# Layer norms with ScalarE's square root and one Newton step, narrower cross scores, a reordered opening and a last block in column pieces

## The chip, the cores and the metric

The kernel runs on 1 core of one Trainium2 chip (trn2). The metric is the device time of one execution in microseconds (us); several executions are taken and their median is given. All tensors are float32 in memory. A matrix product of two float32 operands is made from split operands: a high part `h` rounded to the type float32r, and a low part `l`, the remainder. Three products of float32r (h·h, h·l, l·h) are accumulated in PSUM.

## The reference

A trunk of two post-norm layers over 512 positions of width 1024. Layer 0 mixes tokens with gated linear attention (GLA), layer 1 with gated DeltaNet (GDN); behind each mixer stands a gated feed-forward block with a short causal convolution. After every one of these four sublayers comes a residual and a layer norm:

```python
def layer_norm(x, g, b):
    mu = jnp.mean(xf, -1, keepdims=True)
    var = jnp.mean(jnp.square(xf - mu), -1, keepdims=True)
    return ((xf - mu) * lax.rsqrt(var + LN_EPS)).astype(x.dtype) * g + b
...
    h = layer_norm(ALPHA * h + y, ln_g[i, 0], ln_b[i, 0])
    h = layer_norm(ALPHA * h + conv_ffn(h, ffn_w_in[i], ffn_conv_w[i], ffn_w_out[i]),
                   ln_g[i, 1], ln_b[i, 1])
```

In GLA (4 heads, key width 128, value width 256) the positions are cut into chunks of 64, and the scores of a chunk are `q * exp(b - b_ref)` times `k * exp(b_ref - b)`, causal. The kernel works on pairs of chunks (128 positions), so it also needs the cross scores: queries of the second 64 positions of a pair with keys of the first 64.

## The kernel before

The class `Trunk` holds everything. Positions are cut into 4 blocks of 128 (`tb` 0 to 3, NTB = 4), the width into 8 chunks of 128 (NC = 8) or into two halves of 512 (`hf`, S = 512). The activations lie transposed in `xh` and `xl` (128 partitions x 8 chunks x 512 positions).

**Weights.** `plan` is a list of weight items in the order of their use. `prefetch` issues items up to `look` ahead of the one in use: a DMA on SyncE's queue into one of 3 `raw` buffers, a cast on ScalarE (`wh`, L257), the remainder on VectorE (`wl`, L258). `fm_items` makes products whose outputs have features on the partitions (PSUM tile `fm`), `tm_half` those with positions on the partitions (PSUM tile `tm`): for each pair of weight chunks it goes over the 4 blocks, and the last `tail` pairs it does block by block, so that block 0 is finished while blocks 1 to 3 are still to come. `done` (L393 or L395) then adds the product to the residual `h`, takes the statistics of that half (L400), and after the second half starts the layer norm of the block.

**The order of the work.** The functions are Python generators that are started by `spawn` with a delay and advanced by `pump` between matmuls, on a clock `clk` that the code keeps itself. The framework then orders each engine's instructions by this order and their dependences. `keep_in_program_order` fixes the order of TensorE's instructions until the first mixer's projections are made (`pin`); `behind` puts one instruction after another on the same engine without a wait. `table` chains the activations that need a certain function table of ScalarE in one order, and `exp_ln_table` loads a table ahead of its first use.

**The layer norm.** `ln_stats` (L532 to L546) aggregates the statistics (L534), computes half the variance plus epsilon (L536), a first guess of 1/sqrt by integer instructions (L541, L542), and three Newton steps of two 128x1 instructions (L544, L545). All of it runs on VectorE. `ln` is used by the first three norms: it scales one half of the block on ScalarE (L558) and one on VectorE (L559); TensorE transposes the result (tile `xT`, L175), ScalarE applies gain and bias (`xf`, L568) and the high and low parts are written (L572, L575, L576). `ln_out` is used by the last norm: centering and gain (L600), scaling and bias (L601), the output DMA on SyncE (L602).

**The opening.** `load_x` loads x: blocks 0 and 1 at once on SyncE's and ScalarE's queues, blocks 2 and 3 on ScalarE's queue behind the casts of blocks 0 and 1. TensorE makes 2 constant products (L484) while it waits, transposes blocks 0 and 1 (`x_parts`), and makes 3 more. `fm_items` starts with HEADSTART = 4 weight items on the first 256 positions (blocks 0 and 1), then the same 4 on the other 256. The third of the 4 items is the `rep` item, 16 columns of the gate's low rank (L267, L272, L273). The task `second` transposes blocks 2 and 3 in between. The constants (the norms' weight rows `gla_nw` L728 and `gdn_nw` L938, spread over the partitions, and many small rows, L453) go through GpSimd's queue.

**The cross scores** are made in `core` (L844, tile `sx`): per head and pair of chunks a product of 64 keys with all 128 queries of the pair, of which the columns 64 to 127 are used.

Of the kernel before, what the change touches and what calls it, by code (L numbers as in the profile page):

```python
# [15 lines left out]
P = 128  # L16
# [36 lines left out]
class Trunk:  # L53
# [3 lines left out]
    def __init__(self, ctx, tc):  # L57
        self.tc = tc
        self.nc = nc = tc.nc
        self.n = 0  # L60
        ec = ctx.enter_context
        ap = ec(tc.tile_pool(name="acts", bufs=1))
        self.xh = ap.tile([P, NC, S], F32R, name="xh", tag="xh")
        self.xl = ap.tile([P, NC, S], F32R, name="xl", tag="xl")
        self.wp = ec(tc.tile_pool(name="wts", bufs=WB))
        self.mp = ec(tc.tile_pool(name="mem", bufs=SLOTS))
        self.rp = ec(tc.tile_pool(name="raws", bufs=RAWB))
        self.cp = ec(tc.tile_pool(name="const", bufs=1))
# [6 lines left out]
        self.one, self.warm = ones[:, 0:1], ones[:, 1:2]  # L75
        nc.gpsimd.memset(ones, 1.0)
        self.reset = self.keep([P, S], "reset")
# [9 lines left out]
        self.after = None  # L87
# [8 lines left out]
        self.next_block = 0.0  # L96


# [119 lines left out]
    def issue(self, item):  # L218
# [6 lines left out]
        if item[0] == "fm":  # L225
            _, w, col = item
            nc.sync.dma_start(
                raw.rearrange("p (c f) -> p c f", c=NC),
                w[:, col:col + P].rearrange("(c p) f -> p c f", p=P))
        elif item[0] == "tm":  # L230
# [24 lines left out]
        for n in (S, used) if self.issued == 0 else (used,):  # L255
            cols = slice(0 if n < used or self.issued else S, n)
            nc.scalar.copy(wh[:, cols], raw[:, cols])  # L257
            nc.vector.tensor_sub(wl[:, cols], raw[:, cols], wh[:, cols])  # L258
        self.vec(1.24)
        return [(wh[:, blk(j, S)], wl[:, blk(j, S)]) for j in range(used // S)]  # L260

    def issue_rep(self, w, col):
# [8 lines left out]
        src = r3.unsqueeze(2).to_broadcast([P, NC, 3, 16])  # L271
        nc.scalar.copy(w5[:, :, :, 0, :], src)  # L272
        nc.vector.tensor_sub(w5[:, :, :, 1, :], src, w5[:, :, :, 0, :])  # L273
        return wt

    def prefetch(self):
        while self.issued < min(len(self.plan), self.taken + self.look):
            item = self.plan[self.issued]
            if self.held == WB and not self.in_slots(item):
                break  # L280
            if self.after is None:
                self.ready.append(self.issue(item))
            else:
                with self.tc.issue_after(self.after):
                    self.ready.append(self.issue(item))
                self.after = None
            self.issued += 1
# [67 lines left out]

    def tm_half(self, a, n, tail, done, slots=False):

        npair = (n + 1) // 2
        ps = [self.psum("tm") for _ in range(NTB)]

        def terms(tb, cp, w):
            for j in range(min(2, n - 2 * cp)):
                c = 2 * cp + j
                self.tm_terms(ps[tb], *a(c, tb), *w[j], c == 0, c == n - 1)
            self.pump()
# [7 lines left out]
        for tb in range(NTB):  # L373
            for i in range(tail):
                terms(tb, npair - tail + i, ws[i])
                if tb == NTB - 1 and not slots:
                    self.spend()
            done(tb, ps[tb])

# [3 lines left out]

    def out_proj(self, a, n, first, final):

        nc = self.nc
        self.st = [None] * NTB
        for hf in range(2):
            def done(tb, ps, hf=hf):
                h = self.h[tb][hf]  # L390
                if first:
# [5 lines left out]
                if final is not None:  # L397
                    if hf == 0:
                        self.st[tb] = self.small([P, 2, 6], "ln_st")
                    nc.vector.bn_stats(self.st[tb][:, hf, :], h)  # L400
                    self.vec(0.7)
                    if hf == 1:
# [6 lines left out]
            self.tm_half(a, n, TAIL if last else 1, done, last)  # L409
        self.look = LOOKAHEAD  # L410
# [19 lines left out]
    def split_out(self, dst_h, dst_l, src):  # L430
        cast = self.nc.scalar.copy(dst_h, src)  # L431
        self.nc.vector.tensor_sub(dst_l, src, dst_h)
        return cast

# [27 lines left out]

    def x_parts(self, tb):
        for hf in range(2):
            ps = self.psum("xT")
            self.tr4(ps, self.h[tb][hf])
            xs = (slice(None), slice(4 * hf, 4 * hf + 4), blk(tb))
            cast = self.split_out(self.xh[xs], self.xl[xs], c4(ps))
        self.set(("x", tb))
        return cast.ins  # L470

    def load_x(self, x):
# [18 lines left out]
        constant(2)  # L491
        for tb in range(2):
            cast = self.x_parts(tb)
        constant(3)
        with self.tc.issue_after(cast):
            for tb in range(2, NTB):
                load(nc.scalar, tb)
            self.prefetch()

        def second():  # L500
            for tb in range(2, NTB):
                self.after = self.x_parts(tb)
                yield 1.2
            self.look = LOOKAHEAD

        self.spawn(second(), 4.0)

# [22 lines left out]

    def ln_stats(self, tb):
        nc = self.nc  # L532
        mv = self.small([P, 2], "ln_mv")
        nc.vector.bn_aggr(mv, self.st[tb])  # L534
        hv = self.small([P, 1], "ln_var")
        nc.vector.tensor_scalar(hv, mv[:, 1:2], LN_EPS, 0.5, op0=ALU.add, op1=ALU.mult)  # L536

        rs = self.small([P, 1], "ln_rs")
        t = self.small([P, 1], "ln_t")
        ri = rs.bitcast(I32)  # L540
        nc.vector.tensor_single_scalar(ri, hv.bitcast(I32), 1, op=ALU.logical_shift_right)  # L541
        nc.vector.tensor_scalar(ri, ri, -1.0, float(0x5F3759DF - 0x400000 - (1 << 31)), op0=ALU.mult, op1=ALU.add)  # L542
        for _ in range(3):
            nc.vector.scalar_tensor_tensor(t, rs, hv, rs, ALU.mult, ALU.mult)  # L544
            nc.vector.scalar_tensor_tensor(rs, t, 1.5, rs, ALU.subtract, ALU.mult)  # L545
        self.vec(2.2)  # L546
        return mv, rs
# [47 lines left out]
    def ln_out(self, tb, out):  # L595
        nc = self.nc
        gb, h = self.ln_gb(), self.h[tb]
        mv, rs = self.ln_stats(tb)
        for hf in range(2):
            nc.vector.scalar_tensor_tensor(h[hf], h[hf], mv[:, 0:1], gb[hf], ALU.subtract, ALU.mult)  # L600
            nc.vector.scalar_tensor_tensor(h[hf], h[hf], rs, gb[2 + hf], ALU.mult, ALU.add)  # L601
            nc.sync.dma_start(out[blk(tb), blk(hf, S)], h[hf])  # L602
        yield 0.0
# [49 lines left out]
    def ffn(self, cw, li, g, b, final, out=False):  # L653
        nc = self.nc
        for ci, (f0, f1) in enumerate(CHUNKS):
# [22 lines left out]
            a = lambda c, tb: (gs[c][0][:, blk(tb)], gs[c][1][:, blk(tb)])  # L678
            self.out_proj(a, f1 - f0, ci == 0, final if last else None)

# [37 lines left out]
    def gla_consts(self, w_gk2, b_gk, norm_w):  # L718
# [19 lines left out]
        self.b_gk = self.keep([P, 4], "gla_b")  # L738
        self.spawn(self.columns([(b_gk.rearrange("(n p) -> n p", p=P), 4, self.b_gk)]), 1.0)

    def gla(self, li, g, b):
# [89 lines left out]
        def core(hd):  # L831
# [101 lines left out]
    def gdn_consts(self, conv_w, a_log, dt_bias, norm_w):  # L933
# [460 lines left out]
```

## Time and profile before

| | |
|---|---|
| Median of 3 runs | 1286.5 us (1286.39 to 1287.05) |
| The profiled execution's own time | 1286.57 us |
| Its span, first to last instruction | 1284.5 us |
| TensorE busy (PE) | 1267.5 us, 99% |
| VectorE busy (DVE) | 794.2 us, 62% |
| ScalarE busy (ACT) | 543.8 us, 42% |
| GpSimd busy (POOL) | 111.1 us, 9% |
| Mean DMA rate | 99 GB/s |

Times in the profile count from the start of the span. A row of a timeline has the start, the length, the engine, the line of the kernel, the operation, what it writes and reads, and in brackets how long the engine was idle before it and what ended that. A "q" behind an engine's name means its sequencer, which issues DMAs (SPq, ACTq). A row of groups has the count, then the busy time, the mean length of one in ns, and the engine's idle time ahead of them. A row of the chain has the start, the time until the chain's next piece, and the count. One product of plain float32 operands appears as two matmul records (`sx`, `V`, the constant products), one of float32r operands as one. Matmuls overlap in the pipeline, so a matmul's length is not its cost: the pace is the distance from one start to the next.

### The profile page before, as it was taken

What the parts mean: (1) busy time and instruction counts of PE and PEld (TensorE: products, weight loads), DVE (VectorE), ACT (ScalarE), POOL (GpSimd) and SP (SyncE); (2) the same over time, 40 slices, a digit from 0 to 9 for tenths busy, and PEclk for the clock granted to TensorE, in tenths of its full rate; (3) what the DMA queues carried; (4) which work ended last, traced back from release to release, by engine and by line L of the source; (5) the groups of instructions that cost most, each with busy time, mean ns of one, the idle gap of its engine ahead of it and who ended that gap; (6) DMA issues with size and microseconds to landing.
All of it is one profiled execution on the core that took longest, in us unless ns stands there. A gap on an engine that the chain in (4) does not pass through costs nothing.

```text
span 1284.5 us, 17239 instructions
## 1 busy us (share of the span) xinstructions
PE 1267.5 (99%) x6658; PEld 1069.8 (83%) x6658; DVE 794.2 (62%) x1458; ACT 543.8 (42%) x1030; POOL 111.1 (9%) x150
## 2 busy tenths in 40 slices
PE   9999999999999999999999999999999999999996
PEld 7878888988888888888888888988888888888885
DVE  3853466676643466556789955679687653366657
ACT  3653443634431244425765544542644431244420
POOL 4000000070000000001013120100052000000000
PEclk9999999999999999999999999999999999999998
DMA  6421224143323333351354331234043323333331
GB/s 185 115 83 53 79 83 132 34 131 115 98 90 93 98 97 99 99 150 66 100 149 114 118 76 51 69 113 142 10 150 108 93 91 97 98 98 99 98 99 66
DMA packets 167074, 126.53 MB, mean 99 GB/s; under 512 B 16072, under 2 KB 139530, under 8 KB 166992
## 3 DMA queue, kind: packets, MB, share of 16 engines
q1 hardware_dynamic: 162240, 115.36, 30.3%
q0 software_dynamic: 3888, 8.50, 2.2%
q10 hardware_dynamic: 864, 1.57, 0.4%
q8 instruction: 52, 0.85, 0.3%
q14 instruction: 30, 0.25, 0.1%
HBM read 119.63 MB, written 5.78 MB: 98 GB/s over the span
## 4 chain that ended last, share of the span: by engine, by line
PE 87%; issue 6%; DVE 4%; DMA 1%; POOL 1%; ACT 1%; DVEq 0%; POOLq 0%; ACTq 0%
PE fm L158 47%; PE tm L158 31%; PE o L158 1%; PE R L158 1%; PE V L158 1%; DVE ln_st L400 1%; PE xT L175 1%; PE qkT L175 1%; PE vn L158 1%; PE pq L158 1%; PE pg L158 1%; PE yT L175 1%; DMA gla_nw<-in_gla_norm_w_dram 0%; PE s L158 0%; DVE ln_t L544 0%
## 5 line engine op out<-in xcount | busy, mean ns | idle before, releaser
L258 DVE TENSOR_TENSOR wl<-raw,wh 128x1024 fp32r<-128x1024 f32 (+1 forms) x190 | 238.5, 1257 | 317.0 <-ACT wh L257 316.9
L158 PE MATMUL fm<-xh,wh 128*128 128x512 f32 (+2 forms) x1104 | 404.1, 367 | 0.0
L158 PE MATMUL fm<-xl,wh 128*128 128x512 f32 (+2 forms) x1104 | 401.6, 365 | 0.2 <-DVE xl L576 0.2
L158 PE MATMUL fm<-xh,wl 128*128 128x512 f32 (+1 forms) x1088 | 397.1, 366 | 1.1 <-DVE wl L258 0.9
L257 ACT CAST wh<-raw 128x1024 fp32r<-128x1024 f32 (+1 forms) x190 | 198.9, 1047 | 284.3 <-PE tm L158 165.4
L158 PEld LDWEIGHTS fm<-xh,wh 128*128 128x128 f32 (+1 forms) x1104 | 207.8, 188 | 33.6 <-ACT wh L257 0.8
L158 PEld LDWEIGHTS fm<-xl,wh 128*128 128x128 f32 (+1 forms) x1104 | 207.8, 188 | 32.8 <-DVE xl L576 0.4
L158 PEld LDWEIGHTS fm<-xh,wl 128*128 128x128 f32 x1088 | 204.7, 189 | 34.7 <-DVE wl L258 1.5
L650 DVE SCALAR_TENSOR_TENSOR conv<-fm,ffn_cw,conv 128x511 f32<-128x511 f32 (+1 forms) x176 | 130.8, 746 | 3.0
L158 PE MATMUL tm<-wh,gh 128*128 128x512 f32 x288 | 112.0, 389 | 0.0
L158 PE MATMUL tm<-wl,gh 128*128 128x512 f32 x288 | 112.0, 389 | 0.0
L158 PE MATMUL tm<-wh,gl 128*128 128x512 f32 x288 | 112.0, 389 | 0.0
L431 ACT CAST gh<-conv 128x512 fp32r<-128x512 f32 x44 | 27.3, 622 | 125.0 <-DVE conv L665 124.9
L158 PE MATMUL tm<-wh,xh 128*128 128x512 f32 x192 | 79.5, 414 | 0.1
L158 PE MATMUL tm<-wh,xl 128*128 128x512 f32 x192 | 75.2, 392 | 0.0
L158 PE MATMUL tm<-wl,xh 128*128 128x512 f32 x192 | 75.1, 391 | 0.0
L660 ACT ACTIVATE conv<-conv 128x512 f32<-128x512 f32 x44 | 27.8, 632 | 94.8 <-DVE conv L650 94.7
L158 PEld LDWEIGHTS tm<-wh,gh 128*128 128x128 f32 x288 | 54.1, 188 | 11.3
L158 PEld LDWEIGHTS tm<-wl,gh 128*128 128x128 f32 x288 | 54.1, 188 | 11.3
L158 PEld LDWEIGHTS tm<-wh,gl 128*128 128x128 f32 x288 | 54.1, 188 | 11.1
L648 ACT ACTIVATE conv<-fm,ffn_cw 128x512 f32<-128x512 f32 x88 | 59.9, 681 | 0.2
L950 DVE SCALAR_TENSOR_TENSOR conv<-fm,gdn_cw,conv 128x509 f32<-128x509 f32 (+2 forms) x72 | 53.3, 744 | 4.1 <-ACT conv L948 3.5
(275 smaller groups left out, 1534.3 us busy)
## 6 DMA issues: line engine op xcount, KB each, us to landing
raw<-in_ffn_w_in_dram SPq DMA_DIRECT2D x88, 512.0 KB, 3.7
raw<-in_ffn_w_out_dram SPq DMA_DIRECT2D x44, 512.0 KB, 3.6
raw<-in_gdn_w_in_dram SPq DMA_DIRECT2D x32, 512.0 KB, 4.0
raw<-in_gla_w_in_dram SPq DMA_DIRECT2D x24, 512.0 KB, 3.5
raw<-in_gla_w_out_dram SPq DMA_DIRECT2D x8, 512.0 KB, 3.5
raw<-in_gdn_w_out_dram SPq DMA_DIRECT2D x8, 512.0 KB, 3.7
hd<-h POOLq DMA_DIRECT2D x8, 256.0 KB, 2.5
dt<-drow POOLq DMA_DIRECT2D x8, 256.0 KB, 5.5
```

What stands on the lines that cost most here:

```text
L158: t = self.nc.tensor.matmul(out, a, b, start=start, stop=stop)
L175: t = self.nc.tensor.transpose(out, a, self.ident[:n, :n])
L257: nc.scalar.copy(wh[:, cols], raw[:, cols])
L258: nc.vector.tensor_sub(wl[:, cols], raw[:, cols], wh[:, cols])
L400: nc.vector.bn_stats(self.st[tb][:, hf, :], h)
L431: cast = self.nc.scalar.copy(dst_h, src)
L648: nc.scalar.activation(a, ps, AF.Identity, scale=tap(2))
L650: nc.vector.scalar_tensor_tensor(a[:, d:], ps[:, :S - d], tap(2 - d), a[:, d:], ALU.mult, ALU.add)
L660: nc.scalar.activation(a, a, AF.Gelu)
L950: self.conv = nc.vector.scalar_tensor_tensor(a[:, d:], ps[:, :S - d], tap(3 - d), a[:, d:], ALU.mult, ALU.add)
```

## The change

1. `ln_stats`, for all four norms: ScalarE computes `root = Sqrt(var + eps)` (the bias is a new 128x1 constant `eps`), VectorE its reciprocal and one Newton step on it. The integer guess and two of the three Newton steps are gone. A new function `sqrt_table` loads ScalarE's table before the last half of each output projection. In `ln_out` the centering is placed between the root and the reciprocal.
2. `core`: the cross scores are made with 64 moving columns instead of 128.
3. `tm_half`, `out_proj`, `ln_out`: the very last half projection makes the 512 columns of block 3 in two pieces of 256, each with its own PSUM bank, add and statistics. The second half of block 3 is also written out in two pieces, one on SyncE's queue and one on ScalarE's.
4. The opening: x is split half by half over blocks 0 and 1 instead of block by block; `look` is 2 from the start; the first weight comes in two DMAs; the loads of x blocks 2 and 3 go to SyncE's queue behind the first two weights; 2 constant products instead of 3 follow the transposes; the transposes of blocks 2 and 3 are due later; the splits of the first four weights are ordered behind the last x split; `gla_nw` and `gdn_nw` are loaded after x is done, behind a copy on GpSimd that reads the last `xl`; the GLA bias columns are due at 12.0 instead of 1.0.

```diff
@@ load_x
-        for tb in range(2):
-            cast = self.x_parts(tb)
-        constant(3)
-        with self.tc.issue_after(cast):
-            for tb in range(2, NTB):
-                load(nc.scalar, tb)
-            self.prefetch()
+        for hf in range(2):
+            for tb in range(2):
+                self.first = self.x_part(tb, hf)
+        constant(2)
+        self.look = LOOKAHEAD
+        self.prefetch()
+        for tb in range(2, NTB):
+            load(nc.sync, tb)
...
+            for t, row in self.late:
+                nc.gpsimd.tensor_copy(t[:, :1], self.xl[:, NC - 1, S - 1:].bitcast(F32))
+                nc.gpsimd.dma_start(t, row.partition_broadcast(P))
-        self.spawn(second(), 4.0)
+        self.spawn(second(), 7.0)
@@ issue, the "fm" item
+            step = NC if self.issued else NC // 2
+            for c in range(0, NC, step):
+                nc.sync.dma_start(r3[:, c:c + step, :], w3[:, c:c + step, :])
@@ a new function, called where a weight is split
+    def opening(self, *parts):
+        if self.issued < 4:
+            for ins, other in zip(parts, self.first):
+                self.behind(ins, other)
@@ tm_half
-            for i in range(tail):
-                terms(tb, npair - tail + i, ws[i])
...
-            done(tb, ps[tb])
+            m = len(ps[tb])
+            for piece in range(m):
+                for i in range(tail):
+                    terms(tb, npair - tail + i, ws[i], piece)
...
+                if m == 1:
+                    done(tb, ps[tb][0])
+                else:
+                    done(tb, ps[tb][piece], piece, blk(piece, S // m))
@@ out_proj
             if last:
+                self.sqrt_table()
                 self.look = TAIL + WB
@@ ln_stats
+    def sqrt_table(self):
+        load = self.nc.scalar.preload_act_table_set("sqrt_and_others")
+        self.tc.keep_in_program_order(load)
+        self.table(load)
...
+        root = self.small([P, 1], "ln_root")
+        self.table(nc.scalar.activation(root, mv[:, 1:2], AF.Sqrt, bias=self.eps))
-        nc.vector.tensor_scalar(hv, mv[:, 1:2], LN_EPS, 0.5, op0=ALU.add, op1=ALU.mult)
-        ri = rs.bitcast(I32)
-        nc.vector.tensor_single_scalar(ri, hv.bitcast(I32), 1, op=ALU.logical_shift_right)
-        nc.vector.tensor_scalar(ri, ri, -1.0, float(0x5F3759DF - 0x400000 - (1 << 31)), op0=ALU.mult, op1=ALU.add)
-        for _ in range(3):
-            nc.vector.scalar_tensor_tensor(t, rs, hv, rs, ALU.mult, ALU.mult)
-            nc.vector.scalar_tensor_tensor(rs, t, 1.5, rs, ALU.subtract, ALU.mult)
+        nc.vector.tensor_scalar(hv, mv[:, 1:2], LN_EPS, -0.5, op0=ALU.add, op1=ALU.mult)
+        if center is not None:
+            center(mv)
+        nc.vector.reciprocal(rs, root)
+        nc.vector.scalar_tensor_tensor(t, rs, hv, rs, ALU.mult, ALU.mult)
+        nc.vector.scalar_tensor_tensor(rs, t, 1.5, rs, ALU.add, ALU.mult)
@@ core
-                self.mm(px[:64, blk(ck)], cx[:, ck * P:ck * P + 64], cx[:, blk(ck)])
+                late = slice(ck * P + 64, ck * P + P)
+                self.mm(px[:64, late], cx[:, ck * P:ck * P + 64], cx[:, late])
@@ gla_consts, gdn_consts
-        nc.gpsimd.dma_start(self.gla_nw, norm_w.partition_broadcast(P))
+        self.late.append((self.gla_nw, norm_w))
...
-        nc.gpsimd.dma_start(self.gdn_nw, norm_w.partition_broadcast(P))
+        self.late.append((self.gdn_nw, norm_w))
```

More of the change, by code (lines that the diff above doesn't have):

```diff
@@ L74, in __init__ @@
         ones = self.keep([P, 32], "one")
-        self.one, self.warm = ones[:, 0:1], ones[:, 1:2]
+        self.one, self.warm, self.eps = (ones[:, i:i + 1] for i in range(3))
         nc.gpsimd.memset(ones, 1.0)
+        nc.gpsimd.memset(self.eps, LN_EPS)
         self.reset = self.keep([P, S], "reset")
@@ L96, in __init__ @@
         self.next_block = 0.0
+        self.late = []
+        self.first = None
     def uid(self, s):
@@ L256, in issue @@
             cols = slice(0 if n < used or self.issued else S, n)
-            nc.scalar.copy(wh[:, cols], raw[:, cols])
-            nc.vector.tensor_sub(wl[:, cols], raw[:, cols], wh[:, cols])
+            self.opening(*self.split_out(wh[:, cols], wl[:, cols], raw[:, cols]))
         self.vec(1.24)
@@ L280, in prefetch @@
                 break
[L281 to L286, printed above, removed]
+            self.ready.append(self.issue(item))
             self.issued += 1
@@ L354, in tm_terms, with tm_half, terms @@
         self.mm(ps, al, wh, False, last)
-    def tm_half(self, a, n, tail, done, slots=False):
+    def tm_half(self, a, n, tail, done, slots=False, pieces=1):
         npair = (n + 1) // 2
[L359 to L364, printed above, removed]
+        ps = [[self.psum("tm") for _ in range(pieces if tb == NTB - 1 else 1)] for tb in range(NTB)]
+        def terms(tb, cp, w, piece=None):
+            for i in range(len(ps[tb])) if piece is None else (piece,):
+                cols = blk(i, S // len(ps[tb]))
+                for j in range(min(2, n - 2 * cp)):
+                    c = 2 * cp + j
+                    self.tm_terms(ps[tb][i][:, cols], *a(c, tb), *(t[:, cols] for t in w[j]), c == 0, c == n - 1)
             self.pump()
@@ L382, in x_tm, with out_proj @@
         self.tm_half(a, NC, 1, done)
-    def out_proj(self, a, n, first, final):
+    def out_proj(self, a, n, first, final, pieces=1):
         nc = self.nc
@@ L460, in columns, with x_part @@
             yield 1.0
[L463 to L470, printed above, removed]
+    def x_part(self, tb, hf):
+        ps = self.psum("xT")
+        self.tr4(ps, self.h[tb][hf])
+        xs = (slice(None), slice(4 * hf, 4 * hf + 4), blk(tb))
+        parts = self.split_out(self.xh[xs], self.xl[xs], c4(ps))
+        if hf:
+            self.set(("x", tb))
+        return parts
     def load_x(self, x):
@@ L597, in ln_out, with center @@
         gb, h = self.ln_gb(), self.h[tb]
-        mv, rs = self.ln_stats(tb)
+        def center(mv):
+            for hf in range(2):
+                nc.vector.scalar_tensor_tensor(h[hf], h[hf], mv[:, 0:1], gb[hf], ALU.subtract, ALU.mult)
+        mv, rs = self.ln_stats(tb, center)
         for hf in range(2):
-            nc.vector.scalar_tensor_tensor(h[hf], h[hf], mv[:, 0:1], gb[hf], ALU.subtract, ALU.mult)
-            nc.vector.scalar_tensor_tensor(h[hf], h[hf], rs, gb[2 + hf], ALU.mult, ALU.add)
-            nc.sync.dma_start(out[blk(tb), blk(hf, S)], h[hf])
+            m = 2 if tb == NTB - 1 and hf else 1
+            for i in range(m):
+                cols = blk(i, S // m)
+                nc.vector.scalar_tensor_tensor(h[hf][:, cols], h[hf][:, cols], rs, gb[2 + hf][:, cols],
+                                               ALU.mult, ALU.add)
+                (nc.sync, nc.scalar)[i].dma_start(out[blk(tb), hf * S + cols.start:hf * S + cols.stop],
+                                                  h[hf][:, cols])
         yield 0.0
@@ L678, in ffn @@
             a = lambda c, tb: (gs[c][0][:, blk(tb)], gs[c][1][:, blk(tb)])
-            self.out_proj(a, f1 - f0, ci == 0, final if last else None)
+            self.out_proj(a, f1 - f0, ci == 0, final if last else None, 2 if last and out else 1)
     def split_y(self, y, two, hf, sg):
```

43 lines of the change are left out of this document (19 added, 24 removed).

## The prediction

> **What bounds the kernel now.** I read the page first, then the busy time of each engine by stretch, then who TensorE waited for, then the chain that ended last from 1244 us on, and at the edges the timeline of single engines.
>
> ```profile
> 0.00:25.00 25.00, 21.97 (x128) 17.35 (x129) 10.50 (x15) 9.92 (x16) 14.12 (x33) 1.00 0.86 227
> 25.00:582.00 557.00, 556.55 (x2657) 466.70 (x2656) 320.18 (x509) 229.61 (x360) 28.57 (x21) 1.00 0.32 96
> 582.00:606.00 24.00, 23.61 (x153) 21.10 (x152) 17.17 (x54) 16.42 (x39) 4.14 (x8) 1.00 0.24 88
> 606.00:885.00 279.00, 278.60 (x1916) 240.87 (x1916) 209.89 (x524) 149.48 (x418) 38.42 (x73) 1.00 0.35 99
> 885.00:914.00 29.00, 27.34 (x140) 22.73 (x140) 24.81 (x68) 13.60 (x30) 0.00 (x0) 1.00 0.31 92
> 914.00:1257.00 343.00, 343.00 (x1602) 287.78 (x1602) 188.91 (x228) 124.77 (x168) 25.81 (x16) 1.00 0.32 97
> ```
>
> The columns are the length, the busy time of TensorE, its weight loads, VectorE, ScalarE and GpSimd, the granted clock, the DMA share and GB/s. From 25 us to 1257 us TensorE is idle for 0.45 + 0.39 + 0.40 + 1.66 + 0 = 2.9 us. So inside only two things pay: less TensorE work, and the 0.39 and 1.66 us beside the second and third layer norm. Outside lie the opening and what follows 1257 us. This is who it waits for:
>
> ```profile
> PE xT L175 <- DVE h L559: 1.2, 2, 1.1
> PE fm L158 <- DVE wl L258: 0.9, 1, 0.9
> PE xT L175 <- DVE ln_t L544: 0.6, 1, 0.6
> ```
>
> The first and third rows (1.8 us) are the layer norm's chain on VectorE; the second is a weight of the opening.
>
> **The last block.** Four times VectorE adds the product to the residual (L395), takes the statistics and writes a block out.
>
> ```profile
> L395 DVE TENSOR_TENSOR h<-h,tm x4: 678/680/689, 1257.1 to 1275.1; 128x512 f32<-128x512 f32 x4
> ```
> ```profile
> L600 DVE SCALAR_TENSOR_TENSOR h<-h,ln_mv,gb 128x512 f32<-128x512 f32 x8 | 5.9, 743 | 0.0
> L601 DVE SCALAR_TENSOR_TENSOR h<-h,ln_rs,gb 128x512 f32<-128x512 f32 x8 | 5.7, 748 | 0.1
> L400 DVE BATCH_NORM_STATS2 ln_st<-h 128x6 f32<-128x512 f32 x4 | 2.8, 694 | 0.1
> L395 DVE TENSOR_TENSOR h<-h,tm 128x512 f32<-128x512 f32 x4 | 2.7, 682 | 9.5 <-PE tm L158 9.5
> L544 DVE SCALAR_TENSOR_TENSOR ln_t<-ln_rs,ln_var 128x1 f32<-128x1 f32 x12 | 2.6, 221 | 0.4
> L545 DVE SCALAR_TENSOR_TENSOR ln_rs<-ln_t,ln_rs 128x1 f32<-128x1 f32 x12 | 1.9, 160 | 0.4
> L534 DVE BATCH_NORM_AGGREGATE ln_mv<-ln_st 128x2 f32<-128x12 f32 x4 | 0.8, 208 | 0.1
> L536 DVE TENSOR_SCALAR ln_var<-ln_mv 128x1 f32<-128x1 f32 x4 | 0.6, 155 | 0.1
> L541 DVE TENSOR_SCALAR ln_rs<-ln_var 128x1 int32<-128x1 int32 x4 | 0.6, 148 | 0.0
> L542 DVE TENSOR_SCALAR ln_rs<-ln_rs 128x1 int32<-128x1 int32 x4 | 0.6, 148 | 0.0
> ```
>
> The adds start (1275.1 - 1257.1) / 3 = 6.0 us apart. TensorE needs less for a block, and these two rows of the chain give its pace for 512 and for 256 columns:
>
> ```profile
> 1044.90 65.28 PE tm L158 x288
> ```
> ```profile
> 912.18 5.03 PE fm L158 x42
> ```
>
> 65.28 / 288 = 0.2267 us and 5.03 / 42 = 0.120 us. A block's 24 products take 5.44 us, so VectorE sets the end and loses 0.56 us a block. The change takes two of three steps out of each block: 2 x (0.221 + 0.160 + 0.07 idle) = 0.90 us, and the two integer instructions, 0.30 us, which lie partly under the centerings (L600) and which I count at nothing here. It adds one reciprocal; the nearest rows, 128x1 instructions, take 0.15 to 0.22, so 0.19. A block costs VectorE 6.0 - 0.7 = 5.3 us, below 5.44: it now follows TensorE, up to the last block.
>
> There the columns come in two halves. Thirty products become sixty of half the width: 30 x (2 x 0.120 - 0.2267) = 0.4 us more on TensorE. It had finished block 3 at 1257.1 + 3 x 5.44 = 1273.4; now 1273.8. Behind it VectorE has, for the second half only: add 0.40 and statistics 0.40 (halves of 0.68 and 0.69, plus a fixed part that I put at 0.06), aggregate 0.24, the scaled variance 0.19, two centerings 1.48, reciprocal 0.19, one step 0.45, the first output half 0.75, two quarters 0.80: 4.9 us, so 1278.7. ScalarE's root lies beside the two centerings. Before, the last scaling ended as the last transfer was issued:
>
> ```profile
> L602 SPq DMA_DIRECT2D out_dram<-h x8: 332/333/356, 1262.6 to 1281.2; - x8
> ```
>
> The quarters leave by SyncE and ScalarE, which has nothing else then; a transfer's landing is taken as unchanged. 1281.2 - 1278.7 = **2.5 us** gained. Between ends: 1.6 if half widths cost three quarters of a full one and block 2 is still on VectorE, 3.1 if they cost exactly half and the integer steps count.
>
> **The cross scores.**
>
> ```profile
> 111.81 1.02 PE sx L158 x8
> ```
> ```profile
> 750.58 1.07 PE V L158 x16
> ```
>
> A head's eight records of 128 moving columns take 1.02 us; sixteen 64-column records of the second mixer take 1.07, or 0.54 for eight. The stretch from 25 to 582 us is TensorE's own (0.45 idle in 557), so what is saved there is saved: at most 4 x 0.48 = 1.9. The change of group at the start and end doesn't halve, so I take 4 x 0.40 = **1.6 us**; nothing if the 128-row weights set the pace, which the V row (64 rows) can't exclude.
>
> **The opening.**
>
> ```profile
> 8.59 0.59 ACT L431 CAST xh<-xT 128x512 fp32r<-128x512 f32 x1
> 8.93 1.41 ACTq L479 DMA_DIRECT2D h<-in_x_dram  x3
> 10.38 1.14 ACT L257 CAST wh<-raw 128x512 fp32r<-128x512 f32 x2 [1.20 <-DMA raw<-in_gla_w_in_dram]
> ```
> ```profile
> DMA to landing us min/median/max: 7.9/8.9/10.0
> ```
> ```profile
> 8.35 2.74 PE L484 MATMUL warm<-reset,ident 128*128 128x512 f32 x6
> 11.05 0.39 PE L158 MATMUL fm<-xh,wh 128*128 128x256 f32 x1
> ```
>
> The first weight was asked for at 1.7 us and took 7.9 (first weight transfers, L227), so it lay there at 9.6; the page names the DMA, but ScalarE was issuing x transfers until 10.34. With those on SyncE's queue and the weight in two halves the cast can start when the last x cast ends, at 9.18, or at 9.6 at worst; the first product follows 0.67 us later (10.38 to 11.05). Two warm-up products instead of three end at 8.35 + 1.8 = 10.15. So 10.2 instead of 11.05: -0.85. The Trainium skill's Key Constraints ("Trainium Kernel Development and Optimization") say that another issuing engine saves issue time only; by that all of this 0.85 would be ScalarE's issue time.
>
> Then -0.9 for the opening's wait on wl, and +0.6 for what moves back: the third weight has been queued on SyncE ahead of x blocks 2 and 3 and now stands behind them.
>
> ```profile
> 2.81 3.91 SPq L267 DMA_DIRECT2D raw<-in_gla_w_in_dram  x1
> ```
>
> Four x transfers are 1.05 MB, 4.6 us at the 227 GB/s of the first row; TensorE has two weights' products first, 2 x 24 x 0.120 = 5.8 us. So between 0 and 1.5 us of new wait, 0.6 taken. Sum -1.15, from -2.1 to +0.5. The late norm rows free 0.19 MB (0.8 us of DMA) early, and their reader, the gate at 157 us, hides their delay. They put a copy that waits for the last xl into GpSimd's queue; only constants stand behind it. The added memset, one column, and the later bias column: nothing.
>
> **The three inner norms.** ScalarE's root is not in the trace. Its nearest rows:
>
> ```profile
> L568 ACT ACTIVATE xf<-xT,lb,lg 128x128 f32<-128x128 f32 x32 | 11.6, 467 | 1.0 <-PE xT L175 0.9
> L558 ACT ACTIVATE h<-h,ln_nb,ln_rs 128x512 f32<-128x512 f32 x3 | 2.4, 815 | 5.9 <-DVE ln_nb L557 5.9
> ```
>
> (815 - 467) / 384 = 0.9 ns a column, which leaves 0.35 us for one column. A crossing between engines took 0.1 us in the opening (the first half of the 1.14 us cast ends at 10.95, the product starts at 11.05). So the chain loses 0.90 + 0.30 and gains 0.35 + 0.19 + 2 x 0.1: some 0.5 us shorter, against TensorE's 1.66 + 0.39 us. At the third norm the first wait (0.6) follows one such chain and the second (1.1) at least two in a row; the second norm has 0.39. That makes 0.5 + 1.0 + 0.3, of which I take **1.4 us**, since other VectorE work lies between the chains, and none at the first norm, where TensorE didn't wait. While VectorE waits for the root, its next residual adds, weight remainders and xl remainders are queued behind the reciprocal, and TensorE waits for those; I count nothing because ScalarE is idle at the first two blocks of a norm (5.9 us in the row above).
>
> The four root tables are loaded ahead of each norm's last half. A load in the trace:
>
> ```profile
> 155.86 1.28 ACT L697 ACT_TABLE_LOAD   x1
> 157.15 1.09 ACT L697 ACTIVATE sg<-tm 128x512 f32<-128x512 f32 x2
> ```
>
> It takes 1.28 us and the next instruction starts 0.01 us later. Weight casts wait behind it, whose products are several pairs away: 24 products, 5.44 us, to a pair. I count nothing; without that cover 4 x 1.28 = 5.1 us. The Trainium skill speaks against this: "ScalarE: Activation LUTs", What ACT_TABLE_LOAD costs, budgets about 2.66 us for every switch of set, a drain of 1.38 us added to the load. By that page four switches would hold ScalarE for 10.6 us, not 5.1; the row shows no drain.
>
> **Sum.** -2.5 - 1.6 - 1.4 - 1.15 = -6.65 us. The profiled execution took 1286.57 us, the median of the runs is 1286.5. 1286.57 - 6.65 = **1279.9 us**.
>
> **Rivals.** A, the opening returns nothing: the third weight comes late enough to stall TensorE by the whole gain. For it: 3.91 us of issue for that transfer alone. Against: 0.19 MB fewer ahead. 1281.1 us.
>
> B, slower than before: the root stands in ScalarE's queue behind the previous block's run of xf.
>
> ```profile
> 226.40 2.90 ACT L568 ACTIVATE xf<-xT,lb,lg 128x128 f32<-128x128 f32 x8
> 229.33 0.62 ACT L575 CAST xh<-xf 128x512 fp32r<-128x512 f32 x1
> 230.14 0.82 ACT L558 ACTIVATE h<-h,ln_nb,ln_rs 128x512 f32<-128x512 f32 x1 [0.19 <-DVE ln_nb L557]
> ```
>
> Such a run is 3.5 us, and blocks 2 and 3 of three norms meet one: six chains. At half a run each, TensorE loses 6 x 1.76 = 10.6 us and the 1.4 isn't gained: 1279.9 + 1.4 + 10.6 = 1291.9. It turns the total slower by 0.2% (2.6 us) from (6.65 + 2.6 - 1.4) / 6 = 1.3 us a chain. Against it: the runs aren't kept whole.
>
> ```profile
> 592.31 0.81 ACT L558 ACTIVATE h<-h,ln_nb,ln_rs 128x512 f32<-128x512 f32 x1 [0.18 <-DVE ln_nb L557]
> ```
>
> Here block 2's scaling runs between the first and the other seven xf of block 1.
>
> C, the table switch sits on the chain: if the load runs at the first root and not ahead, three inner norms pay 1.28 each, and the last block's 0.14 us of slack a block takes 0.4 of a fourth: 1279.9 + 3 x 1.28 + 0.9 = 1284.6. By the Trainium skill's 2.66 us (the page and section above) it would be 1290.1.
>
> D, the cross scores don't get cheaper: 1281.5.
>
> **How the numbers follow.** Within 0.2%, about 2.6 us, a measurement here can't tell a change from none. My forecast 0.66, A 0.10 and D 0.08 are faster by more, together 0.84. C 0.06, and A and D with a short tail together 0.04, lie within it: 0.10. B 0.06 is slower. The range goes from 1276.5 (opening -2.1, scores -1.9, norms -2.05, end -3.1, and 0.85 from the two 0.4 us waits that no edit aims at) to 1284.3 (A, D, the end's 1.6 and half of the norms' gain); B and the dear end of C stay out.
>
> **What would show it.** Right: first weight product near 10.2 us; sx groups of about 0.6 us; no wait of xT on h at the third norm above 0.3 us; the last adds at TensorE's pace, 5.4 us apart, and the last transfer issued near 1278.7 less what came before, that is near 1274.5. Wrong: VectorE idle before the reciprocal with ScalarE's xf as its releaser (B), a table load between aggregate and root (C), TensorE waiting on the third weight (A), sx groups still near 1.0 us (D).

## The result and the profile after

The changed kernel takes 1278.1 us (median of 6 runs, 1277.93 to 1278.55), the kernel before 1286.55 us beside it (6 runs, 1286.27 to 1287.05). The ratio is 0.9935 with a 95% interval from 0.9924 to 0.9945: 8.45 us less, where 6.65 had been predicted. The span went from 1284.5 to 1276.2 us.

Where the 8.3 us of span went is read by following the same piece of TensorE's work through both traces. Four such markers are these; before first (a row of the timeline, then the chain that ended last):

```profile
65.52 1.05 PE L158 MATMUL sa<-e,e 128*128 128x128 f32 x8
...
364.53 65.28 PE tm L158 x288
...
602.62 19.39 PE fm L158 x156
...
1044.90 65.28 PE tm L158 x288
```

After, the same four:

```profile
63.09 1.05 PE L160 MATMUL sa<-e,e 128*128 128x128 f32 x8
...
360.79 65.28 PE tm L160 x288
...
599.33 17.94 PE fm L160 x144
...
1039.17 65.28 PE tm L160 x288
```

The first is the start of the first head's scores: 2.43 us earlier, all from the opening. The second is the first feed-forward's output projection, behind the first mixer and the first norm: 3.74 earlier, so 1.31 more. The third ends (start plus length) at 622.01 and 617.27, behind the second norm: 1.00 more. The fourth lies behind the third norm: 5.73, so 0.99 more. The last transfer is issued at 1272.89 instead of 1281.2, so the end gave 2.58.

| stretch | predicted | traces |
|---|---|---|
| opening, to 63 us | -1.15 | -2.43 |
| cross scores, 63 us to the first norm | -1.6 | -1.31 |
| first norm | 0 | 0 |
| second and third norm | -1.4 | -1.99 |
| last block | -2.5 | -2.58 |
| sum | -6.65 | -8.3 |

Cross scores and first norm lie between the same two markers. That all of the 1.31 is the scores' is read from `s1_norms` below, the kernel before with the new norms alone: there the two markers are 299.2 us apart (65.56 to 364.79), 299.0 before, so the first norm gave nothing.

Two of TensorE's waits after, by what it waited for (us in total, times, longest):

```profile
PE xT L177 <- DVE ln_mv L557: 0.9, 1, 0.9
PE kt L177 <- DVE sc L872: 0.8, 1, 0.8
```

The opening's 0.9, a wait for the remainder of the fourth weight, is gone, and of the waits of xT (1.2 and 0.6) one of 0.9 is left. A new one stands in the second row, which no step of the prediction had. The busy time by stretch (length, then TensorE, its weight loads, VectorE, ScalarE, GpSimd):

```profile
25.00:580.00 555.00, 554.07 (x2646) 464.60 (x2645) 318.01 (x488) 235.66 (x375) 29.51 (x22) 1.00 0.32 97
580.00:602.00 22.00, 22.00 (x147) 20.09 (x146) 13.89 (x37) 14.13 (x36) 3.97 (x7) 1.00 0.19 72
602.00:878.00 276.00, 275.61 (x1900) 238.29 (x1899) 208.14 (x520) 150.49 (x419) 38.51 (x73) 1.00 0.35 99
878.00:906.00 28.00, 27.12 (x131) 22.45 (x130) 23.25 (x50) 13.10 (x27) 0.00 (x0) 1.00 0.34 99
906.00:1250.00 344.00, 344.00 (x1622) 289.23 (x1621) 190.30 (x229) 128.17 (x176) 25.85 (x16) 1.00 0.32 97
```

TensorE's idle time from 25 to 1250 us is 0.93 + 0 + 0.39 + 0.88 + 0 = 2.2 us. At the second norm nothing is left of 0.39, at the third 0.88 of 1.66, and in the first stretch it rose from 0.45 to 0.93, by the new wait.

**The norm's chain.** One undisturbed chain on VectorE, before and after:

```profile
214.27 0.21 DVE L534 BATCH_NORM_AGGREGATE ln_mv<-ln_st 128x2 f32<-128x12 f32 x1
...
216.44 0.16 DVE L557 SCALAR_TENSOR_TENSOR ln_nb<-ln_mv,ln_rs 128x1 f32<-128x1 f32 x1
```
```profile
210.56 0.21 DVE L557 BATCH_NORM_AGGREGATE ln_mv<-ln_st 128x2 f32<-128x12 f32 x1
210.80 0.15 DVE L561 TENSOR_SCALAR ln_var<-ln_mv 128x1 f32<-128x1 f32 x1
211.13 0.16 DVE L565 RECIPROCAL ln_rs<-ln_root 128x1 f32<-128x1 f32 x1 [0.17 <-ACT ln_root L559]
...
211.77 0.16 DVE L579 SCALAR_TENSOR_TENSOR ln_nb<-ln_mv,ln_rs 128x1 f32<-128x1 f32 x1
```

From aggregate to `ln_nb` it was 2.17 us and is 1.21: 0.96 shorter, not 0.5. ScalarE's root, which this row of ScalarE's timeline shows, starts with the scaled variance at 210.80 and takes 0.29; the reciprocal waits only 0.17 for it.

```profile
210.80 0.29 ACT L559 ACTIVATE ln_root<-ln_mv,one 128x1 f32<-128x1 f32 x1 [6.08 <-DVE ln_mv L557]
```

**The end.** The chain that ended last, from TensorE's last product on, and the issue of the last output transfer:

```profile
1268.09 0.43 DVE h L401
...
1271.31 0.75 DVE h L630
```
```profile
L632 ACTq DMA_DIRECT2D out_dram<-h x1: 353/353/353, 1272.9 to 1272.9; - x1
```

From TensorE's last piece (1268.07) to the last issue it is 4.8 us; 4.9 was predicted. The adds of the four blocks run from 1251.5 (first of the row below) to 1262.34 for the third: 5.4 us apart, as predicted, and they now wait for TensorE.

```profile
L401 DVE TENSOR_TENSOR h<-h,tm x5: 399/686/689, 1251.5 to 1268.1; 128x512 f32<-128x512 f32 x3, 128x256 f32<-128x256 f32 x2
```
```profile
1262.34 0.69 DVE L401 TENSOR_TENSOR h<-h,tm 128x512 f32<-128x512 f32 x1 [0.30 <-PE tm L160]
```

### The profile page after: what moved, and what is told of

The parts are those of the page before. It is cut to its first block, busy times and chain, and to the rows that moved or that the text cites. A ratio compares the mean times of both kernels' runs of the same rounds, so it can differ in the third digit from the quotient of the medians.

```text
span 1276.2 us, 17247 instructions
## 1 busy us (share of the span) xinstructions
PE 1263.8 (99%) x6686; PEld 1070.0 (84%) x6686; DVE 783.5 (61%) x1381; ACT 552.8 (43%) x1050; POOL 111.1 (9%) x153
## 4 chain that ended last, share of the span: by engine, by line
PE 94%; DVE 3%; ACT 1%; issue 1%; DMA 0%; POOL 0%; DVEq 0%; ACTq 0%; POOLq 0%
PE fm L160 50%; PE tm L160 35%; PE o L160 2%; PE xT L177 1%; PE R L160 1%; PE V L160 1%; PE qkT L177 1%; PE vn L160 1%; PE pq L160 1%; PE pg L160 1%; PE yT L177 1%; DVE wl L438 1%; PE s L160 0%; PE warm L495 0%; PE qs L160 0%
```

## The experiments

Twelve kernels ran, in three series, each in 5 rounds beside the kernel before: 1286.83, 1286.63 and 1286.94 us.

### One part at a time

Each of the first four is the kernel before with one part of the change: `s1_norms` the new `ln_stats`, the table loads and the centering between root and reciprocal; `s2_scores` the 64 columns; `s3_tail` the pieces; `s4_opening` the opening.

> The kernel before with the new norm alone (root, one step, table ahead, centering between root and reciprocal). Theory: TensorE loses its waits at the second and third norm (about 1.0 us each, as in the changed kernel), and at the end VectorE needs 5.0 us a block and not 6.0, so that the end follows TensorE: 2.0 + 2.4 = 4.4 us less than before, about 1282.1. Rival 1, the end's gain comes from the column pieces: only 2 us less, about 1284.5. Rival 2, the root stands behind runs of xf: no gain or slower.

1282.12 us, ratio 0.996 (0.9947 to 0.9972): 4.7 less. The last transfer's row shows what that does at the end:

```profile
L613 SPq DMA_DIRECT2D out_dram<-h x8: 332/332/356, 1260.2 to 1277.2; - x8
```

The eight issues now span 17.0 us, where they spanned 18.6 before (1262.6 to 1281.2), without any piece. The end's gain belongs to the norms.

> The kernel before with the cross scores of 64 columns alone. Theory: TensorE saves 4 x 0.41 = 1.6 us, but for the first heads VectorE sets the pace, and a wait of TensorE's kt on the mask copy takes 0.8 us back: 0.8 us less, about 1285.7. Rival, the saving is whole: 1.6 us less, about 1284.9. Second rival, narrower products cost the same: no change, sx groups still 1.0 us.

1285.47 us, ratio 0.9988 (0.9979 to 0.9997): 1.4 less, with 0.4 to 2.7 inside the interval, so this run alone doesn't separate the two. Its trace has the new wait of 0.8 us (kt on the masked copy), so the wait comes with the narrower scores and nothing else.

> The kernel before with the last block's column pieces alone (two PSUM banks, two adds and statistics, the last output half in two pieces). Theory: VectorE is 1.8 us behind TensorE when the last block comes, so halves change little: the shorter last output piece saves 0.3, one more add and statistics cost 0.1 to 0.2 and TensorE's 0.4 is hidden: between 0 and 0.3 us less, about 1286.4. Rival, the pieces carry the end's gain: 2 us or more less, 1284.5 or lower.

1287.19 us, ratio 1.0001 (0.9992 to 1.001): nothing that these runs can tell, with 1.0 less to 1.3 more inside the interval. While VectorE needs 6.0 us a block, pieces of TensorE's work don't matter.

> The kernel before with the new opening alone (order of x, queues, two halves of the first weight, late norm rows and bias columns, two constant products). Theory: first product 1.05 us earlier, the two waits on wl (1.2 us) gone, and the later wait on a row load (0.4) too: 2.4 to 2.9 us less, about 1283.9. Rival, as the prediction had it: 1.15 us less, about 1285.4, with a wait on the third weight.

1284.21 us, ratio 0.9979 (0.997 to 0.9988): 2.6 less, twice what the prediction gave the opening. The four singles sum to -4.7 - 1.4 + 0.4 - 2.6 = -8.3, the whole is -8.45. Each single's interval is 1.0 to 1.6 us to either side; within that the parts don't help or hinder each other.

### Root, table, pieces, scores

`m1_guess` is the changed kernel without the root: the integer guess is back, with one Newton step: two Newton steps are left out and nothing takes their place. It parts the gain of fewer steps from the price of the root.

```diff
-        root = self.small([P, 1], "ln_root")
-        self.table(nc.scalar.activation(root, mv[:, 1:2], AF.Sqrt, bias=self.eps))
...
-        nc.vector.reciprocal(rs, root)
+        nc.vector.tensor_single_scalar(ri, hv.bitcast(I32), 1, op=ALU.logical_shift_right)
...
+        nc.vector.tensor_scalar(ri, ri, -1.0, float(0x5F3759DF - 0x400000 - (1 << 31)), op0=ALU.mult, op1=ALU.add)
```

> The changed kernel with the old integer first guess and one step instead of the root (two Newton steps are left out, so its norm is coarser; no table load, no crossing to ScalarE). Theory: what pays in the norms are the two dropped steps, and the root costs a chain as much as the two integer instructions: same time as the changed kernel within 0.4 us, 1277.7 to 1278.5. Rival, the root's way over ScalarE costs the norms: 1 us or more less, 1277.1 or lower. Opposite rival, the root is what pays: 1 us or more over the changed kernel, 1279.1 or higher.

1278.35 us, ratio 0.9936 (0.9923 to 0.9948): the same. Root, reciprocal and the crossing to ScalarE and back together cost no more than two integer instructions; what pays is the two steps that are gone. An undisturbed chain there takes 1.41 us from the start of the aggregate to the end of `ln_nb`, and 1.38 in the changed kernel.

`m2_nopre` is the changed kernel without the four early table loads, which was to put them on the chain (rival C).

```diff
             if last:
-                self.sqrt_table()
                 self.look = TAIL + WB
```

> The changed kernel without the explicit table loads, so that a load comes where the first root needs it. Theory (rival C of the prediction): the 1.28 us load stands between the first block's statistics and its root. The third norm, where TensorE already waits 0.9 us for that chain, pays all of it; the first and second have some slack: 2 to 4 us over the changed kernel, 1280 to 1282. Rival, the load is hidden anyway: within 0.4 us of 1278.1.

1278.30 us, ratio 0.9935 (0.9923 to 0.9948): the same, and my expectation fell. ScalarE's timeline around the first norm's first root says why:

```profile
203.66 1.05 ACT L437 CAST wh<-raw 128x1024 fp32r<-128x1024 f32 x1 [2.01 <-PE tm L160]
204.73 1.28 ACT L558 ACT_TABLE_LOAD   x1
210.79 0.29 ACT L558 ACTIVATE ln_root<-ln_mv,one 128x1 f32<-128x1 f32 x1 [4.78 <-DVE ln_mv L556]
```

The load belongs to the root's line, but it didn't wait for the root's operand: it began 0.02 us after the cast ahead of it and ended 4.8 us before the aggregate came. The other three do the same (568.61, 890.70 and 1231.64 us, each right behind a cast), though not all with that margin: the third norm's load ends 0.8 us before its root. The early loads bring nothing, since the switch finds ScalarE idle.

`m3_nopieces` makes the last half product of block 3 in one piece of 512 again; its output still leaves in pieces.

```diff
-            self.out_proj(a, f1 - f0, ci == 0, final if last else None, 2 if last and out else 1)
+            self.out_proj(a, f1 - f0, ci == 0, final if last else None)
```

> The changed kernel with the last block's product in one piece of 512 columns (the output still leaves in the new pieces). Theory: with VectorE following TensorE the pieces matter now: the add and statistics of 512 columns stand behind TensorE's end, 0.65 us more, less the 0.4 us that TensorE saves: 0.2 to 0.5 us over the changed kernel, about 1278.4. Rival, the pieces carry the end's gain: 2 us over it, about 1280.

1278.27 us, ratio 0.9936 (0.9923 to 0.9948): the pieces bring at most 0.2 us, which these runs can't tell from nothing.

`m4_wide` puts the 128 columns back into the changed kernel.

```diff
-                late = slice(ck * P + 64, ck * P + P)
-                self.mm(px[:64, late], cx[:, ck * P:ck * P + 64], cx[:, late])
+                self.mm(px[:64, blk(ck)], cx[:, ck * P:ck * P + 64], cx[:, blk(ck)])
```

> The changed kernel with cross scores of 128 columns again. Theory: TensorE's work grows by 1.65 us but its 0.8 us wait of kt on VectorE goes: 0.8 us over the changed kernel, about 1278.9, and kt no longer waits. Rival, the wait has another cause and stays: 1.6 us over, about 1279.7.

1279.71 us, ratio 0.9947 (0.9933 to 0.996), beside 1278.27 to 1278.35 for its three neighbours: the narrower scores are worth 1.4 us, not 0.8. The second head's key transposes show where a part of it went. With 128 columns, and after:

```profile
70.73 0.66 PE L177 MATMUL kt<-ident,e 128*128 128x128 f32 x4
```
```profile
70.69 0.66 PE L177 MATMUL kt<-ident,e 128*128 128x128 f32 x4 [0.82 <-DVE sc L872]
```

They start at the same time, although two groups of scores ahead of them are shorter by 0.41 us each. The masked copy on VectorE holds them:

```profile
69.94 0.70 DVE L872 COPY_PREDICATED sc<-gla_mask,sa 128x512 f32<-128x512 uint8 x1
```

So what the first two heads save is waited away; the third and fourth, at 108 to 114 us, keep theirs, another 0.8. Of the remaining 0.6, 0.45 is a wait that `m4_wide` has and the changed kernel hasn't:

```profile
86.19 0.63 PE L177 MATMUL cols<-ident,rows 96*128 96x96 f32 x3 [0.45 <-DMA rows<-in_gdn_conv_w_dram]
```

With wide scores the code's own clock puts the group of columns ahead of this one, which frees its rows' buffer, six products earlier; the rows then took 2.8 us to land, 2.0 with the narrow scores. That this wait hangs on the width only by the order of the work is read from the two traces; it wasn't tried by itself.

### The opening, taken apart, and one try at a faster kernel

`o1_xq` puts x blocks 2 and 3 back on ScalarE's queue.

```diff
-        self.prefetch()
         for tb in range(2, NTB):
-            load(nc.sync, tb)
+            load(nc.scalar, tb)
+        self.prefetch()
```

> The changed kernel with x blocks 2 and 3 back on ScalarE's queue, issued before the weights are asked for, so that the third weight's transfer again stands ahead of them in SyncE's queue. Theory: four transfers of about 0.47 us of issue each hold ScalarE ahead of the first weight's cast; the first product comes 0.9 us later than 10.23 and the wait for the first weight's remainder comes back, nothing is won by the earlier third weight: 1279.2 (1278.8 to 1279.6). Rival (the third weight behind four x blocks costs TensorE the 0.6 us that the prediction took): the two cancel and the time stays within 0.4 us of 1278.2.

1281.25 us, ratio 0.9956 (0.9943 to 0.9968): 3.1 us more than `o3_whole` beside it, far over both numbers. ScalarE's timeline:

```profile
4.70 4.70 ACTq L490 DMA_DIRECT2D h<-in_x_dram  x3
9.45 2.05 ACT L438 CAST xh<-xT 128x512 fp32r<-128x512 f32 x4 [6.23 <-PE warm L495]
```

Without the order behind the casts that the kernel before had, the four issues went ahead of them, and three took 4.7 us, not the 1.41 of the kernel before. The x casts stood behind them until 9.45 (6.67 after), and TensorE had nothing to do for 2.92 us ahead of its first weight product. Then a second loss follows. The stretches from 12 us on (columns as above, the granted clock ahead of the last two):

```profile
12.00:14.00 2.00, 1.93 (x10) 1.93 (x11) 1.75 (x3) 1.15 (x3) 0.45 (x2) 0.57 1.09 232
14.00:15.70 1.70, 1.70 (x10) 1.70 (x9) 1.23 (x1) 1.36 (x3) 0.00 (x0) 0.50 0.35 80
15.70:18.00 2.30, 2.30 (x21) 2.30 (x21) 1.24 (x2) 0.41 (x1) 0.00 (x0) 1.00 0.96 272
```

After the pause the clock is granted at half until 15.7 us: 16 products, from 12.07 to 15.48, start 0.21 us apart instead of 0.12, 1.5 us in all. The second product starts 2.06 us later than in the changed kernel (12.29 for 10.23); with the 1.5 that is 3.6. By the start of the first head's scores 3.3 of it is left (66.35 for 63.09), and the median shows 3.1. This shows what DMA issues cost in ScalarE's queue, more than was in question; it doesn't tell the third weight's 0.6 from nothing, because TensorE was late anyway. The Trainium skill's Key Constraints ("Trainium Kernel Development and Optimization"), cited in the prediction, agree in kind: what another issuing engine saves is issue time.

`o2_rows` loads the two norm rows at the start again.

```diff
-        self.late.append((self.gla_nw, norm_w))
+        nc.gpsimd.dma_start(self.gla_nw, norm_w.partition_broadcast(P))
...
-        self.late.append((self.gdn_nw, norm_w))
+        nc.gpsimd.dma_start(self.gdn_nw, norm_w.partition_broadcast(P))
```

> The changed kernel with the two norm rows loaded at the start again (two transfers on GpSimd's queue, 0.19 MB). Theory: these rows compete with the first weights for the DMA engines; the second weight lands later than 11.0 us, TensorE waits for it or its remainder by 0.4 to 1.0 us, and the time is 1278.6 to 1279.2. Rival (early DMA traffic isn't what the first weights wait for): unchanged, 1278.2 within 0.3.

1279.05 us, ratio 0.994 (0.9927 to 0.9952): 0.9 more than its neighbours `o3_whole` and `f1_later`, whose five runs each end at 1278.33 or lower, while these begin at 1278.5, as the theory had it. TensorE waits for the second weight and for its remainder:

```profile
12.70 0.39 PE L160 MATMUL fm<-xh,wh 128*128 128x256 f32 x1 [0.58 <-ACT wh L438]
13.96 0.39 PE L160 MATMUL fm<-xh,wl 128*128 128x256 f32 x1 [0.76 <-DVE wl L438]
```

The second weight's cast starts at 11.60 instead of 11.05. The two waits aren't the loss itself, for the first weight product came earlier here, at 8.87 us for 9.80, and TensorE only waited longer behind it. The loss is that the second weight's remainder is first used at 13.96 instead of 13.41; the first head's scores start at 63.73, 0.64 behind the changed kernel and 0.85 behind `o3_whole` (62.88).

`o3_whole` asks for the first weight in one transfer.

```diff
-            step = NC if self.issued else NC // 2
+            step = NC
```

> The changed kernel with the first weight in one transfer instead of two halves. Theory: the weight had landed by 9.6 us at the latest, so the first cast starts up to 0.5 us later than 9.11: 1278.5 (1278.2 to 1278.8). Rival (the halves are what brings the start forward): first product at 10.9 or later and 1279.0 or more.

1278.14 us, ratio 0.9933 (0.9921 to 0.9946): no difference. The halves bring nothing: the first cast started at 9.01 us, and by the account of the opening below the first weight isn't what TensorE is held up by.

`f1_later` was meant to beat both kernels by moving the key transposes later.

```diff
-            yield 0.8
+            yield 2.4
             pk = self.psum("kt")
```

> The changed kernel with each head's key transposes one group of six products (1.36 us) later in TensorE's order, behind the cross scores, so that the masked copy on VectorE is done when they come. Theory: the new 0.8 us wait of the key transposes goes and nothing takes its place: 1277.4 (1277.2 to 1277.7), faster than both kernels. Rival (the wait is VectorE's backlog, which whatever comes next meets as well): the wait moves to another row and the time stays within 0.3 us of 1278.2.

1278.11 us, ratio 0.9932 (0.9919 to 0.9946): no difference, and no test of the idea. The edit moved the transposes of the third and fourth head; those of the second, which wait, stayed behind the same products, with the same wait of 0.83 us at 70.77. Whether the wait can be filled stays open.

## Why the prediction was right, step by step

**The bound.** That TensorE bounds the kernel and that only less TensorE work, its waits and the two ends pay held: every term of the table lies there. Each term but one came out larger or equal, which is why the total is 1.8 us better than forecast; the opening makes 1.3 of that.

**The last block: mechanism and size right, the part named for it half wrong.** Two Newton steps less put VectorE below TensorE's 5.44 us a block, and `s1_norms` shows that this alone brings the end in. The pieces, for which 0.4 us of TensorE time was paid, return that and no more (`s3_tail`, `m3_nopieces`).

**The inner norms: right in place, sizes wrong both ways.** The chain is 0.96 us shorter, not 0.5. The term that failed is the root's: 0.35 us and two crossings of 0.1 were put in series, but the root runs beside the scaled variance, and of 0.29 us only 0.17 shows. The same size of the root can be read beside the Trainium skill, "ScalarE: Activation LUTs", What ACT_TABLE_LOAD costs: about 280 ns for an activation with a bias in memory, before the columns; the trace's 0.29 agrees.

The prediction's 0.5 + 1.0 for the third norm came out at 0.99 and its 0.3 for the second at 1.00, so the sum is 1.99 where 1.8 was added up and 1.4 taken: two errors against each other, partly luck. At the second norm it took the 0.39 us that the profile shows as idle for all that could be won. From start to start the stalls there were larger: two products started 0.50 and 0.45 us behind the one ahead (597.62 and 601.53 us) instead of 0.12, 0.7 together, with 0.22 and 0.17 shown as idle.

That the shorter chain alone took these waits away isn't shown. The change also lowers what the code's own clock charges for the chain (`self.vec` in `ln_stats`, from 2.2 to 1.4), and with it TensorE's order changed in every kernel with the new norms: most of the transposes come six products earlier, those of block 3 at the second norm 12 later, those of block 2 at the third norm 18 later. By the trace after, the two old places would have met their operand within 0.1 us (596.73 for an operand done at 596.82, 905.40 for 905.39), so by this estimate the chain would have done nearly all of it; no run parts the two.

The sign "no wait of xT above 0.3 us at the third norm" was wrong: 0.9 is left, and 0.9 to 1.3 in the other kernels with the new norms. The first of the two waits there didn't go: block 0's statistics stand behind a weight remainder that waits for its cast, not behind a norm's chain.

```profile
890.56 1.23 DVE L438 TENSOR_TENSOR wl<-raw,wh 128x1024 fp32r<-128x1024 f32 x1 [1.19 <-ACT wh L438]
891.70 0.69 DVE L406 BATCH_NORM_STATS2 ln_st<-h 128x6 f32<-128x512 f32 x1
```

TensorE's order also has those transposes six products earlier than before, so the shorter chain meets an earlier reader.

**The cross scores: the price right, the cover missed.** 0.41 us a head was saved, as taken (0.40). "What is saved there is saved" failed: TensorE has no idle time there, but VectorE's masked copy was due within 0.1 us of when TensorE needed it (70.64 us by the row above, and the wide kernel's transposes come at 70.73). Half of the gain became a wait, and a good half of that came back where the columns no longer wait.

**The opening: the mechanism missed, the size too small.** By the prediction's terms, the second product started at 11.28 us before and at 10.23 after, 1.05 earlier (0.85 predicted). The waits on weight remainders fell by 1.2 us, counted from start to start over the pace of 0.12 (1.39 to 0.20), not 0.9. The third weight, cast from 14.81, is first used at 16.15 without a wait: the 0.6 us came out at nothing, and rival A with it.

But the start doesn't set the length of the opening. `m2_nopre` has the opening of the changed kernel, and its first weight product came 1.2 us earlier still, at 8.61 for 9.80; then TensorE waited for the second weight's remainder up to the same time. `m2_nopre`, then the changed kernel:

```profile
8.61 0.49 PE L160 MATMUL fm<-xh,wh 128*128 128x256 f32 x1
...
13.44 0.39 PE L160 MATMUL fm<-xh,wl 128*128 128x256 f32 x1 [0.76 <-DVE wl L437]
```
```profile
13.41 0.39 PE L160 MATMUL fm<-xh,wl 128*128 128x256 f32 x1
...
16.15 0.28 PE L160 MATMUL fm<-xh,wh 128*96 128x256 f32 x1
```

The first head's scores start at 63.11 and 63.09 us. With the old opening it is the same: `s1_norms` made its second product at 10.47, 0.8 earlier than the kernel before, and its scores start at 65.56, not earlier than 65.52.

What set the old opening was the fourth weight; the 0.9 us was a wait for its remainder. ScalarE and TensorE before:

```profile
18.13 0.62 ACT L725 CAST gk<-gk 96x512 fp32r<-96x512 f32 x1 [1.06 <-DMA gk<-in_gla_w_gk_dram]
18.65 1.54 ACT L431 CAST xh<-xT 128x512 fp32r<-128x512 f32 x3
20.08 1.06 ACT L257 CAST wh<-raw 128x1024 fp32r<-128x1024 f32 x1
```
```profile
22.63 0.39 PE L158 MATMUL fm<-xh,wl 128*128 128x256 f32 x1 [0.94 <-DVE wl L258]
```

ScalarE stood until `gk`, the weight of the gate, had landed; casts of x blocks 2 and 3 came behind that, and the fourth weight's cast behind them. It starts at 20.1 to 20.4 us in all four kernels with the old opening. ScalarE after:

```profile
11.05 1.05 ACT L438 CAST wh<-raw 128x1024 fp32r<-128x1024 f32 x1 [0.78 <-DMA raw<-in_gla_w_in_dram]
12.00 0.62 ACT L756 CAST gk<-gk 96x512 fp32r<-96x512 f32 x1
14.81 0.51 ACT L275 CAST wh<-raw 128x384 fp32r<-128x384 f32 x1 [2.19 <-DMA raw<-in_gla_w_in_dram]
16.62 1.05 ACT L438 CAST wh<-raw 128x1024 fp32r<-128x1024 f32 x1 [1.30 <-DMA raw<-in_gla_w_in_dram]
```

The loads of `gk` are now issued from 1.9 us on GpSimd's queue, not from 9.9 behind the row loads, and the x casts come behind the fourth weight's. The prediction took the 0.9 us off without saying which weight it was or what would free it, so that this term came out is luck. The later bias columns, one candidate for what let `gk` go first, it put at nothing; no run changes them alone. The norm rows aren't what held `gk`: in `o2_rows`, where they are loaded at the start, its loads still go first and its cast starts at 12.55. What the rows cost is the second weight's landing, 0.9 us by `o2_rows`; the prediction only counted them as freeing 0.8 us of DMA.

**The rivals.** B's mechanism is there, but small. Two roots, of block 2 at the first and at the third norm, stood behind a whole run. The first:

```profile
221.57 2.90 ACT L590 ACTIVATE xf<-xT,lb,lg 128x128 f32<-128x128 f32 x8
224.33 0.33 ACT L559 ACTIVATE ln_root<-ln_mv,one 128x1 f32<-128x1 f32 x1
```

Its reciprocal came 1.1 us later than in an undisturbed chain, yet VectorE filled the time with remainders and was idle for 0.43; the other's came 1.5 us later, with 0.42 idle. Over all inner chains the tile's own row gives the reciprocal's idle time:

```profile
  ACT ln_root L559: 2.7, 12
```

0.22 us each, beside 0.17 without any queue and the 1.3 from which B would decide. C needs a load that waits for the root; `m2_nopre` shows that it doesn't, and that its cover holds even without the early loads. Behind two of the four new loads in the trace after the next cast starts within 0.02 us (at 191.36 and 868.65). The Trainium skill's drain of 1.38 us on top (the same page and section) isn't seen there: the trace decides. D is refuted by the groups of 0.6 us and by `m4_wide`.

## What to carry to other kernels

An engine that is never idle still doesn't keep all that is saved on it: ask for the next reader when its operand is ready, for here half of a gain ended in a copy that had come just in time. Price a chain that spreads over two engines by what runs beside it, not by the sum of its instructions. And before paying for finer pieces at the end, look which engine paces the last blocks: once VectorE's steps were gone, the pieces had nothing left to win. At a start, follow a later piece of work through the traces, not the first one: here the first product could come a microsecond earlier and nothing behind it moved.

## What was not expected of the hardware

A table load ahead of an activation doesn't wait for that activation's operand: in `m2_nopre` the first ended 4.8 us before the root began, the third 0.8. DMA issues on ScalarE's queue took 0.47 us each in the kernel before and 1.57 in `o1_xq`, where they held its casts for 2.8 us; why an issue took three times as long there isn't shown. And a pause of TensorE of 2.9 us was followed by 3.4 us at half the clock (`o1_xq`, 12.1 to 15.5 us), in the one profiled execution that has such a pause. That speaks for keeping TensorE busy with the opening's constant products, which compute nothing, until the first weight is there; no run leaves them out.
